# When the 64-column products with V are issued: two attention stages of a diffusion trunk on one core

## The chip, the cores and the metric

The kernel runs on one core of one Trainium2 chip. Its time is the time of the whole program on the device in microseconds (us). The kernel before took 2924.12 us, the median of 3 runs (2918.45 to 2926.39).

## The reference, cut to what matters

Two transformer layers work on 1024 latent tokens and 256 context tokens of width 1024, all in float32. Each layer has an attention mixer and a gated feed-forward part. Layer 0 has windowed attention with 16 query heads that share 4 key heads, layer 1 has neighbourhood attention with 16 heads and a bias. In both, the head width is 64, and the part that the change touches is the last line, p times V:

```
# layer 0: a block of 128 queries sees 3 blocks of latent keys and the 256 context keys
s = einsum('bqhgd,bkhd->bhgqk', q_b, k_b) * scale
p = softmax_f32(where(valid, s, NEG_INF), sink_g)
o = einsum('bhgqk,bkhd->bqhgd', p, v_b)
# layer 1: the same with a window in two dimensions and a bias on the scores
s_lat = einsum('bjqhd,bjkhd->bhjqk', q_b, k_s) * scale + bias
s_ctx = einsum('bjqhd,bkhd->bhjqk', q_b, k_c) * scale
p = softmax_f32(where(valid, concatenate([s_lat, s_ctx], -1), NEG_INF))
o = einsum('bhjqk,bjkhd->bjqhd', p[..., :nkey], v_s) + einsum('bhjqk,bkhd->bjqhd', p[..., nkey:], v_c)
```

## The kernel before, in words

The program has five stages, one after the other: projections of layer 0 (`front0`), its attention (`attn0`), output projection and feed-forward part (`back`), the projections of layer 1 (`front1`), its attention (`attn1`), and `back` again. The change touches the two attentions. Everything outside them is products of 128 by 128 weights.

Both attentions work through units. A unit of the first one is a key head g and a block b of 128 queries, with the four query heads that share that key head: 4 times 10 units. A unit of the second one is a pair of heads and a block m of 128 queries: 8 times 8 units. A unit goes through four steps:

- `begin` loads the queries of the unit into a buffer (`qst`). The first attention has 2 such buffers and uses one a unit, with four DMAs (L543, L544). The second one loads two query blocks at a time, for the two heads apart, into 3 buffers (L679 to L682); a load waits until the scores have read what the buffer held. All these DMAs go out in order on SyncE's queue, among the loads of keys, V, bias and weights.
- `scores` multiplies queries and keys into two banks of PSUM (L555 and L557; L697 and L700), of which there are two pairs. VectorE adds mask or bias and takes the minimum (L564; L705), which frees the banks, and ScalarE takes the exponential (L569; L707).
- `turn` transposes the exponentials on TensorE, 128 keys at a time (L588; L725), and copies the result from PSUM to SBUF on VectorE or ScalarE in turn (L509 or L511) into a tile `pt` or `ptt`.
- `finish` multiplies those tiles by V (L598; L740). V has 64 columns a head, so such a product fills half the columns of TensorE; a product for the upper 64 rows of the output and one for the lower 64 stand beside each other in the code. The trace has two MATMUL records for each of these products. After them the reciprocals of the sums are turned to the same layout (L601; L746), the result is scaled and split into two parts for the output projection.

The units overlap: in one turn of the loop the code writes the scores of unit u, the transposes of the unit before it (`prev`), and then `finish`, in the first attention of `prev`, in the second of the unit before `prev` (`old`).

The order on each engine is not the order of the code. A scheduler builds it when the program is built: among the instructions whose inputs are ready by its own reckoning it takes the one written first. `tc.high_priority(offset=n)` lets what stands in it count as if it were written n instructions earlier; the scores have 10 and 20 (HP0, HP1). So the products of `finish` are dealt out one by one where the scheduler finds room between transposes and scores. On the chip each engine follows its list in order and waits where an input is late.

Of the kernel before, what the change touches and what calls it, by code (L numbers as in the profile page):

```python
# [11 lines left out]
F32 = mybir.dt.float32  # L12
# [7 lines left out]
P = 128  # L20
# [9 lines left out]
EPS = 1e-6  # L30
HP0 = 10
HP1 = 20
MB1 = 1
ST, SB = "sq", 1
SP = ((1, 0), (0, 1))
# [13 lines left out]
def f32(ap):  # L49
    return ap.bitcast(F32)  # L50


class Trunk:
# [459 lines left out]
    def attn0(self):  # L513
        nc, tc, a = self.nc, self.tc, self.a
        with ExitStack() as cx:
# [2 lines left out]
            cx.enter_context(self.early)  # L518
            pool = self.early_pool
            late = self.pool(cx, "at0l", 1)  # L520
            prt = lambda: late.tile([P, 640], F32, name="pr0", tag="pr0", bufs=9)
            ptile = lambda: late.tile([P, 512], F32, name="pt", tag="pt", bufs=8)
            o = [self.pair_tiles(c) for c in range(3)]
            mask, mask7 = (self.slot(F32).rearrange("p a n -> p (a n)")[:, :n] for n in (640, 512))
            sink = pool.tile([P, HEADS], F32, name="sink", bufs=1)
# [5 lines left out]
            def load_g(g):  # L531
                kst = pool.tile([P, T], F32R, name="kst")
                for i in range(2):
                    nc.sync.dma_start(out=f32(kst[64 * i:64 * i + 64]), in_=f32(self.ks[0][g * 64:(g + 1) * 64, i, :]))
                v = pool.tile([P, 10, DH], F32, name="vg")
                nc.sync.dma_start(out=v, in_=self.vs[0][0, :, g * 64:(g + 1) * 64].rearrange("(t p) d -> p t d", p=P))
                return kst, v

            def begin(g, b, kst, v):
                q = pool.tile([P, 2, 4, P], F32R, name="qst", tag="qst", bufs=2)  # L540
                for i in range(2):
                    s = f32(self.qs[0][g * 256:(g + 1) * 256, i, b * P:(b + 1) * P]).rearrange("(h d) t -> d h t", d=DH)
                    nc.sync.dma_start(out=f32(q[0:64, i]), in_=s)  # L543
                    nc.sync.dma_start(out=f32(q[64:128, i]), in_=s)  # L544
                lat = list(range(max(b - 1, 0), min(b + 2, 8))) if b < 8 else []
                return dict(g=g, b=b, kst=kst, v=v, q=q, kts=lat + [8, 9], nl=len(lat) * P, p=[], pt=[],
                            sm=self.small.tile([P, 4], F32, name="sm"), mn=self.small.tile([P, 4], F32, name="mn4"))
# [37 lines left out]
            def turn(u, i):  # L585
                tp = self.bank()
                for h in range(4):
                    nc.tensor.transpose(tp[:, h * P:(h + 1) * P], u["p"][h][:, i * P:(i + 1) * P], self.ident)  # L588
                pt = ptile()
                self.evac(pt, tp)  # L590
                u["pt"].append(pt)

            def finish(u):
                g, b, kts = u["g"], u["b"], u["kts"]
                op = self.bank()
                for i, kt in enumerate(kts):
                    for r in range(2):
                        nc.tensor.matmul(op[64 * r:64 * r + 64, :256], u["v"][:, kt, :], u["pt"][i][:, 256 * r:256 * r + 256],  # L598
                                         start=(i == 0), stop=(i == len(kts) - 1))
                for x in range(2):  # L600
                    nc.tensor.transpose(op[:, 256 + x * P:256 + (x + 1) * P], u["rx"][:, x * P:(x + 1) * P], self.ident)  # L601
                ot = late.tile([P, 256], F32, name="ot0", tag="ot0")
                nc.scalar.copy(out=ot, in_=op[:, 256:512])
                nc.vector.tensor_tensor(out=ot, in0=op[:, :256], in1=ot, op=ALU.mult)  # L604
                if b < 8:
                    ov = ot.rearrange("p (x m j) -> p x m j", x=2, m=8)
                    for c in range(2):
                        oh, ol = (o[c][i][g].rearrange("p x (m t) -> p x m t", t=P)[:, :, :, b * 16:b * 16 + 16]
                                  for i in range(2))
                        sv = ov[:, :, 4 * c:4 * c + 4]  # L610
                        nc.gpsimd.tensor_copy(out=oh, in_=sv)
                        nc.gpsimd.tensor_tensor(out=ol, in0=sv, in1=f32(oh), op=ALU.subtract)
                else:
                    oh, ol = (o[2][i][g][:, :, (b - 8) * P:(b - 7) * P] for i in range(2))
                    sv = ot.rearrange("p (x j) -> p x j", x=2)
                    nc.gpsimd.tensor_copy(out=oh, in_=sv)
                    nc.gpsimd.tensor_tensor(out=ol, in0=sv, in1=f32(oh), op=ALU.subtract)

            prev = None
            for g in range(4):  # L620
                kst, v = load_g(g)
                for b in ORD:
                    if WB(g, b):
                        self.wo_ahead.append(self.unit(a["w_o0"][len(self.wo_ahead)], LO, after=prev["rx"] if len(self.wo_ahead) < 2 else None))
                    u = begin(g, b, kst, v)
                    n = len(prev["kts"]) if prev else 0
                    for j in range(max(4, n)):
                        if j < 4:
                            with tc.high_priority(offset=HP0):
                                scores(u, j)  # L630
                        if j < n:
                            turn(prev, j)
                    if g == 0 and b == RB:
                        self.rest(ptile)
                    if prev:
                        finish(prev)
                    prev = u
            for j in range(len(prev["kts"])):
                turn(prev, j)
            finish(prev)  # L640
        return o

    def attn1(self):
        nc, tc, a = self.nc, self.tc, self.a
        with ExitStack() as cx:
# [3 lines left out]
            late = self.pool(cx, "at1l", 1)  # L649
            prt = lambda: late.tile([P, 640], F32, name="pr1", tag="pr1", bufs=4)  # L650
# [39 lines left out]
            def scores(u, x):  # L690
# [19 lines left out]
                if m % 2 == 1 and x == 1:  # L710
# [5 lines left out]
                    u["rx"] = rx  # L716
                    if m == MB1:
                        cur["rx"] = rx
# [12 lines left out]
            def finish(u):  # L731
                pr, m, kts = u["pr"], u["m"], u["kts"]
                if m % 2 == 0:
                    u["two"]["op"] = self.bank()
                op = u["two"]["op"]
                ov = op[:, (m % 2) * P:(m % 2) * P + P]
                n = len(kts)
                for i in range(n):
                    for x in range(2):
                        nc.tensor.matmul(ov[64 * x:64 * x + 64, :], u["v"][:, kts[i], 64 * x:64 * x + 64],  # L740
                                         u["pt"][i // 2][:, (2 * (i % 2) + x) * P:(2 * (i % 2) + x + 1) * P],
                                         start=(i == 0), stop=(i == n - 1))
                if m % 2 == 0:
                    return
                for y in range(2):
                    nc.tensor.transpose(op[:, 256 + y * P:256 + (y + 1) * P], u["rx"][:, y * P:(y + 1) * P], self.ident)  # L746
                ot = late.tile([P, 256], F32, name="ot1", tag="ot1")
                nc.scalar.copy(out=ot, in_=op[:, 256:512])
                nc.vector.tensor_tensor(out=ot, in0=op[:, :256], in1=ot, op=ALU.mult)
                c0 = (m % 4 - 1) * P  # L750
                oh, ol = (o[m // 4][i][pr // 2][:, pr % 2, c0:c0 + 256] for i in range(2))
                nc.scalar.copy(out=oh, in_=ot)
                nc.gpsimd.tensor_tensor(out=ol, in0=ot, in1=f32(oh), op=ALU.subtract)

            old = prev = None
            for pr in range(8):
                load_pair(pr)
                for m in range(8):
                    if m % 2 == 1 and pr == 7:
                        self.wo_ahead.append(self.unit(a["w_o1"][len(self.wo_ahead)]))  # L760
                    u = begin(pr, m)
                    steps = list(range(0, len(prev["kts"]), 2)) if prev else []
                    for j in range(max(2, len(steps))):
                        if j < 2:
                            with tc.high_priority(offset=HP1):
                                scores(u, j)
                        if j < len(steps):
                            turn(prev, steps[j])
                    if old:
                        finish(old)  # L770
                    old, prev = prev, u
            for i in range(0, len(prev["kts"]), 2):
                turn(prev, i)
            finish(old)
            finish(prev)
        return o

# [498 lines left out]
```

## Time and profile before

| | |
|---|---|
| time of the profiled execution | 2916.41 us |
| its span, from the first to the last instruction | 2914.6 us |
| TensorE (PE) busy | 2840.7 us, 97% of the span, 15586 MATMUL records |
| VectorE (DVE) busy | 1642.0 us, 56% |
| ScalarE (ACT) busy | 1123.9 us, 39% |
| GpSimd (POOL) busy | 790.9 us, 27% |
| granted TensorE clock, mean | 0.994 |
| first attention | about 278 to 548 us of the span |
| second attention | about 1883 to 2149 us |

A MATMUL record reaches from its start to the modelled end of its result; neighbours overlap, so a busy share of 97% says that TensorE is nearly always at something, not that it is at its peak. What a stream of products costs is read from the distance between starts.

### The profile page before, as it was taken

The page shows a single profiled execution, that of the slowest core. Times are in us where ns is not written, and L with a number is a line of the kernel's source. Part 1 is how long each engine was busy: PE and PEld are TensorE (multiplying, and loading weights), DVE is VectorE, ACT ScalarE, POOL GpSimd, SP SyncE. Part 2 cuts the span into 40 slices and gives each one's busy share as a digit, 9 for nine tenths or more (in the row PEclk, how much of TensorE's full clock was granted, in tenths as well). Part 3 has the DMA queues.
Part 4 walks back from the last instruction along what each step waited for, and adds up shares of the span by engine and source line. Part 5 has one row for each costly group of instructions (what it writes and reads, how often), then busy time and mean ns, then how long its engine had stood idle before and what let it go on. Part 6 is the DMA issues. An engine that isn't in the chain of part 4 may idle for free.

```text
span 2914.6 us, 42716 instructions
## 1 busy us (share of the span) xinstructions
PE 2840.7 (97%) x15586; PEld 2303.1 (79%) x15586; DVE 1642.0 (56%) x2965; ACT 1123.9 (39%) x2263; POOL 790.9 (27%) x802
## 2 busy tenths in 40 slices
PE   6999999999999999999999999999999999999999
PEld 3667777787888887778998888777788788887887
DVE  5667777558665644446543444266656965566442
ACT  4323666435232322224543223266644522233120
POOL 3443242110122122233872345011101021223220
PEclk8999999999999999999999999999999999999999
DMA  7573342433322258544552554356654422226221
GB/s 267 191 233 95 98 130 73 164 110 131 127 85 86 76 176 287 179 160 140 186 185 89 148 160 127 110 158 158 180 171 136 145 91 82 85 85 204 87 91 62
DMA packets 306178, 404.18 MB, mean 139 GB/s; under 512 B 30128, under 2 KB 165808, under 8 KB 305968
## 3 DMA queue, kind: packets, MB, share of 16 engines
q1 hardware_dynamic: 237072, 362.91, 39.3%
q10 hardware_dynamic: 68896, 38.55, 4.6%
q8 instruction: 123, 2.02, 0.3%
q14 instruction: 87, 0.71, 0.1%
HBM read 317.73 MB, written 83.62 MB: 138 GB/s over the span
## 4 chain that ended last, share of the span: by engine, by line
PE 86%; DVE 3%; DMA 2%; issue 1%; POOL 1%; ACT 1%; SPq 0%; DVEq 0%; ACTq 0%; POOLq 0%
PE b L802 16%; PE bm L1062 16%; PE bm L802 11%; PE bm L352 11%; PE bm L860 7%; PE bm L1123 4%; PE b L598 3%; PE b L588 3%; PE b L740 2%; PE b L1062 2%; PE b L725 2%; PE b L352 2%; DMA qst<-q_s 1%; PE b L555 1%; PE b L697 1%; PE b L700 1%
## 5 line engine op out<-in xcount | busy, mean ns | idle before, releaser
L1062 PE MATMUL bm<-pr,wsp 128*128 128x512 f32 x1920 | 440.3, 390 | 0.0
L1062 PEld LDWEIGHTS bm<-pr,wsp 128*128 128x128 f32 x1920 | 359.3, 188 | 82.0 <-issue 5.9
L802 PE MATMUL b<-wsp,px 128*128 128x512 f32 x1584 | 377.2, 391 | 0.0
L802 PEld LDWEIGHTS b<-wsp,px 128*128 128x128 f32 x1584 | 297.5, 188 | 65.1
L802 PE MATMUL bm<-pr,px 128*128 128x512 f32 x1296 | 316.6, 392 | 5.4 <-ACT kp L964 5.2
L842 DVE SCALAR_TENSOR_TENSOR px<-bm,mod,px 128x512 f32<-128x512 f32 (+1 forms) x232 | 170.3, 739 | 268.4 <-PE bm L1062 219.7
L141 ACT CAST wsp<-raw 128x512 fp32r<-128x512 f32 x306 | 188.0, 620 | 341.1 <-PE bm L1062 122.2
L802 PEld LDWEIGHTS bm<-pr,px 128*128 128x128 f32 x1296 | 243.3, 188 | 59.7 <-ACT kp L964 6.1
L352 PE MATMUL bm<-wsp,pr 128*128 128x512 f32 x1152 | 272.4, 393 | 0.0
L142 POOL TENSOR_TENSOR px<-wt,px 128x512 fp32r<-128x512 f32 x64 | 91.3, 1427 | 626.6 <-ACT px L141 383.4
L352 PEld LDWEIGHTS bm<-wsp,pr 128*128 128x128 f32 x1152 | 213.4, 188 | 43.4
L142 POOL TENSOR_TENSOR wsp<-raw,wsp 128x512 fp32r<-128x512 f32 x132 | 174.9, 1333 | 249.0 <-ACT wsp L141 224.5
L141 ACT CAST px<-wt 128x512 fp32r<-128x512 f32 x176 | 107.9, 621 | 334.5 <-PE b L802 301.8
L142 DVE TENSOR_TENSOR wsp<-raw,wsp 128x512 fp32r<-128x512 f32 x174 | 140.4, 812 | 145.7 <-ACT wsp L141 145.5
L860 PE MATMUL bm<-pr,wsp 128*128 128x512 f32 x768 | 176.8, 390 | 1.0 <-DVE ot L604 1.0
L860 PEld LDWEIGHTS bm<-pr,wsp 128*128 128x128 f32 x768 | 143.3, 188 | 30.5 <-DVE ot L604 1.2
L352 PE MATMUL b<-wsp,pr 128*128 128x512 f32 x576 | 149.3, 414 | 18.3 <-ACT pr L261 6.6
L705 DVE CUSTOM_DVE_ANT_0 pr<-b,wsp,big 128x640 f32<-128x640 f32 (+1 forms) x128 | 107.4, 846 | 87.1 <-PE b L700 86.0
L352 PEld LDWEIGHTS b<-wsp,pr 128*128 128x128 f32 x576 | 110.9, 198 | 55.6 <-issue 9.9
L292 POOL TENSOR_TENSOR hrs<-hss,mhalf 128x8 f32<-128x8 f32 (+1 forms) x66 | 104.7, 1586 | 167.7 <-DVE hss L290 162.8
L1160 DVE TENSOR_TENSOR t<-b,kp 128x512 f32<-128x512 f32 x88 | 60.7, 690 | 135.3 <-PE b L802 133.9
L1123 PE MATMUL bm<-prc,wsp 128*128 128x256 f32 x1056 | 134.2, 285 | 0.0
(205 smaller groups left out, 4834.7 us busy)
## 6 DMA issues: line engine op xcount, KB each, us to landing
raw<-w_gu SPq DMA_DIRECT2D x156, 256.0 KB, 2.8
qst<-q_s SPq DMA_DIRECT2D x288, 128.0 KB, 3.1
rawf<-w_gu SPq DMA_DIRECT2D x132, 256.0 KB, 3.0
raw<-w_down SPq DMA_DIRECT2D x110, 256.0 KB, 3.3
wsp<-w_ada SPq DMA_DIRECT2D x48, 512.0 KB, 7.0
pr<-w_ada SPq DMA_DIRECT2D x48, 512.0 KB, 6.4
s_s<-t SPq DMA_DIRECT2D x88, 256.0 KB, 2.0
rawf<-s_s SPq DMA_DIRECT2D x88, 256.0 KB, 3.1
```

What stands on the lines that cost most here:

```text
L141: self.nc.scalar.copy(out=w[:, 0, :n], in_=x)
L142: getattr(self.nc, lo).tensor_tensor(out=w[:, 1, :n], in0=x, in1=f32(w[:, 0, :n]), op=ALU.subtract)
L292: nc.gpsimd.tensor_tensor(out=rs[:, :nh], in0=ss[:, :nh], in1=self.mhalf[:, :nh], op=ALU.pow)
L352: self.nc.tensor.matmul(ps, x, y, start=(k == 0 and i == 0), stop=(k == KT - 1 and i == 2))
L588: nc.tensor.transpose(tp[:, h * P:(h + 1) * P], u["p"][h][:, i * P:(i + 1) * P], self.ident)
L598: nc.tensor.matmul(op[64 * r:64 * r + 64, :256], u["v"][:, kt, :], u["pt"][i][:, 256 * r:256 * r + 256], start=(i == 0), stop=(i == len(kt ...
L705: nc.vector.tensor_tensor_reduce(out=pt[:, :nl + 256], in0=V, in1=u["bias"][x][m // 7][:, b0:b0 + nl + 256], scale=-1.0, scalar=self.big, ...
L802: self.nc.tensor.matmul(ps, x, y, start=first and k == 0 and i == 0, stop=last and k == 3 and i == 2, skip_group_check=True)
L842: nc.vector.scalar_tensor_tensor(out=h[c, k], in0=ps, scalar=mod[:, ty, k, z:z + 1], in1=h[c, k], op0=ALU.mult, op1=ALU.add)
L860: nc.tensor.matmul(ps[:, :n], x, y, start=(k == 0 and i == 0), stop=(k == KT - 1 and i == 2))
L1062: nc.tensor.matmul(ps, x, y, start=(z == 0 and i == 0), stop=(z == len(parts) - 1 and i == 2))
L1123: nc.tensor.matmul(ps[:, q * CTX:(q + 1) * CTX], x, y, start=(k == 0 and i == 0), stop=(k == KT - 1 and i == 2))
```

## The change

There are four parts.

- In the first attention the products with V of a unit stand in `high_priority(offset=HV0)` with HV0 = 0.
- `finish` of the first attention comes one unit later, as in the second one (`done`), and at the end two of them follow each other. As the tiles `pt` live one unit longer, there are 10 of them and not 8; of the tiles with exponentials (`pr0`) there are 8 and not 9.
- In the second attention the products stand in `high_priority(offset=HV1)` with HV1 = 100.
- There the blocks of keys are taken in reverse, the last one first.

Number and shapes of all instructions stay as they were.

```
-            prt = lambda: late.tile([P, 640], F32, name="pr0", tag="pr0", bufs=9)
-            ptile = lambda: late.tile([P, 512], F32, name="pt", tag="pt", bufs=8)
+            prt = lambda: late.tile([P, 640], F32, name="pr0", tag="pr0", bufs=8)
+            ptile = lambda: late.tile([P, 512], F32, name="pt", tag="pt", bufs=10)
...
-                for i, kt in enumerate(kts):
-                    for r in range(2):
-                        nc.tensor.matmul(op[64 * r:64 * r + 64, :256], u["v"][:, kt, :], u["pt"][i][:, 256 * r:256 * r + 256],
-                                         start=(i == 0), stop=(i == len(kts) - 1))
+                n = len(kts)
+                with tc.high_priority(offset=HV0):
+                    for i in range(n):
+                        for r in range(2):
+                            nc.tensor.matmul(op[64 * r:64 * r + 64, :256], u["v"][:, kts[i], :], u["pt"][i][:, 256 * r:256 * r + 256],
+                                             start=(i == 0), stop=(i == n - 1))
...
-                    if prev:
-                        finish(prev)
-                    prev = u
+                    if done:
+                        finish(done)
+                    done, prev = prev, u
             for j in range(len(prev["kts"])):
                 turn(prev, j)
+            finish(done)
             finish(prev)
...
-                for i in range(n):
-                    for x in range(2):
-                        nc.tensor.matmul(ov[64 * x:64 * x + 64, :], u["v"][:, kts[i], 64 * x:64 * x + 64],
-                                         u["pt"][i // 2][:, (2 * (i % 2) + x) * P:(2 * (i % 2) + x + 1) * P],
-                                         start=(i == 0), stop=(i == n - 1))
+                with tc.high_priority(offset=HV1):
+                    for i in reversed(range(n)):
+                        for x in range(2):
+                            nc.tensor.matmul(ov[64 * x:64 * x + 64, :], u["v"][:, kts[i], 64 * x:64 * x + 64],
+                                             u["pt"][i // 2][:, (2 * (i % 2) + x) * P:(2 * (i % 2) + x + 1) * P],
+                                             start=(i == n - 1), stop=(i == 0))
```

What the scheduler makes of it is seen on TensorE. In the rows of an order, b is a bank of PSUM, pt and ptt are transposed exponentials, pr holds exponentials, vg and v hold V, ident is the identity of a transpose, and rx the reciprocals; x8 says that eight such instructions follow each other. The first place is on TensorE in the first attention, the last query block of the first key head, whose eight products go into one bank (b_3360 before). Before:

```order
L598 MATMUL b_3360<-pt,vg 64x256 x4
L588 MATMUL b_3393<-ident,pr_3297 128x128
L588 MATMUL b_3393<-ident,pr_3312 128x128
L598 MATMUL b_3360<-pt,vg 64x256 x2
L588 MATMUL b_3408<-ident,pr_3297 128x128
L588 MATMUL b_3408<-ident,pr_3312 128x128
L555 MATMUL b_3385<-kst,qst 128x384 x2
...
L588 MATMUL b_3408<-ident,pr_3327 128x128
L598 MATMUL b_3360<-pt,vg 64x256 x2
L601 MATMUL b_3360<-ident,rx_3244 128x128 x2
```

And now the same unit (its bank is b_3435, and line 598 is line 602 of the changed kernel):

```order
L590 MATMUL b_3428<-ident,pr_3322 128x128
L557 MATMUL b_3397<-kst,qst 128x384 x2
L559 MATMUL b_3397<-kst,qst 128x256 x2
L557 MATMUL b_3412<-kst,qst 128x384 x2
L559 MATMUL b_3412<-kst,qst 128x256 x2
L602 MATMUL b_3435<-pt,vg 64x256 x8
L605 MATMUL b_3435<-ident,rx_3232 128x128 x2
```

The three groups of four, two and two products have become one of eight, and the reciprocals follow at once.

The second place is on TensorE in the second attention, between two score products: L700 into b_19629 is the last to read a query buffer, and L697 into b_19710 is the first that needs what is loaded into that buffer. Before:

```order
L700 MATMUL b_19629<-kst_19457,qst_19576 128x384 x2
L740 MATMUL b_19620<-ptt,v_19455 64x128 x8
L697 MATMUL b_19645<-kst_19466,qst_19579 128x256 x2
L700 MATMUL b_19645<-kst_19466,qst_19579 128x384 x2
L725 MATMUL b_19638<-ident,pr_19589 128x128
L740 MATMUL b_19620<-ptt,v_19455 64x128 x4
L725 MATMUL b_19658<-ident,pr_19589 128x128
L740 MATMUL b_19620<-ptt,v_19455 64x128 x3
L725 MATMUL b_19665<-ident,pr_19589 128x128
L740 MATMUL b_19620<-ptt,v_19455 64x128 x2
...
L740 MATMUL b_19620<-ptt,v_19455 64x128
...
L697 MATMUL b_19710<-kst_19466,qst_19690 128x256 x2
```

And now:

```order
L705 MATMUL b_19629<-kst_19457,qst_19576 128x384 x2
L746 MATMUL b_19620<-ptt,v_19455 64x128 x8
L702 MATMUL b_19645<-kst_19466,qst_19579 128x256 x2
L705 MATMUL b_19645<-kst_19466,qst_19579 128x384 x2
L730 MATMUL b_19638<-ident,pr_19589 128x128
L730 MATMUL b_19658<-ident,pr_19589 128x128
L746 MATMUL b_19620<-ptt,v_19455 64x128 x10
...
L752 MATMUL b_19620<-ident,rx_19552 128x128 x2
L702 MATMUL b_19710<-kst_19466,qst_19690 128x256 x2
```

The same eighteen products stand between the two score products in two groups and not in five, and no group has an odd number.

In the whole program the 336 products of the first attention stand in 105 groups before and in 48 now, the 608 of the second in 130 before and 67 now. Groups with an odd number of products: none before and 16 now in the first, 54 before and none now in the second. Outside the attentions some sixty instructions of each `back` change places with neighbours of the same kind.

## Rows read from the trace of the kernel before

**Rows 1.** The page: busy time of each engine, share of the span, instructions

```profile
PE 2840.7 (97%) x15586; PEld 2303.1 (79%) x15586; DVE 1642.0 (56%) x2965; ACT 1123.9 (39%) x2263; POOL 790.9 (27%) x802
```

**Rows 2.** By stretch: us; busy PE, PEld, DVE, ACT, POOL (records); clock; DMA share, GB/s

```profile
278.00:548.00 270.00, 264.91 (x1950) 194.38 (x1950) 195.91 (x548) 184.98 (x483) 82.74 (x195) 1.00 0.34 96
1883.00:2149.00 266.00, 257.79 (x2362) 207.33 (x2360) 171.20 (x407) 169.84 (x408) 38.14 (x86) 0.99 0.59 155
2112.80:2117.00 4.20, 4.19 (x36) 3.85 (x36) 2.14 (x4) 1.78 (x6) 0.73 (x1) 0.59 0.51 176
```

**Rows 3.** Timeline of TensorE, first attention: start, duration, records, waits in brackets

```profile
339.71 1.08 PE L598 MATMUL b<-pt,vg 128*64 128x256 f32 x8
340.73 0.44 PE L588 MATMUL b<-ident,pr 128*128 128x128 f32 x2
341.10 0.65 PE L598 MATMUL b<-pt,vg 128*64 128x256 f32 x4
341.68 0.44 PE L588 MATMUL b<-ident,pr 128*128 128x128 f32 x2
```

**Rows 4.** Timeline of TensorE and one query load, second attention

```profile
2018.53 1.09 PE L740 MATMUL b<-ptt,v 128*64 128x128 f32 x16
2018.63 0.52 SPq L681 DMA_DIRECT2D qst<-q_s  x1
...
2019.55 0.51 PE L697 MATMUL b<-kst,qst 128*128 128x256 f32 x2
...
2020.25 0.27 PE L725 MATMUL b<-ident,pr 128*128 128x128 f32 x1
2020.45 0.66 PE L740 MATMUL b<-ptt,v 128*64 128x128 f32 x8
...
2021.04 0.33 PE L725 MATMUL b<-ident,pr 128*128 128x128 f32 x1
2021.30 0.65 PE L740 MATMUL b<-ptt,v 128*64 128x128 f32 x6
...
2021.88 0.33 PE L725 MATMUL b<-ident,pr 128*128 128x128 f32 x1
2022.14 0.44 PE L740 MATMUL b<-ptt,v 128*64 128x128 f32 x4
2022.51 0.39 PE L697 MATMUL b<-kst,qst 128*128 128x256 f32 x1
2022.73 0.93 PE L725 MATMUL b<-ident,pr 128*128 128x128 f32 x7
2023.41 0.36 PE L697 MATMUL b<-kst,qst 128*128 128x256 f32 x1
...
2024.06 0.43 PE L740 MATMUL b<-ptt,v 128*64 128x128 f32 x2
2024.43 0.44 PE L746 MATMUL b<-ident,rx 128*128 128x128 f32 x2
2026.25 0.47 PE L697 MATMUL b<-kst,qst 128*128 128x256 f32 x2 [1.39 <-DMA qst<-q_s]
```

**Rows 5.** Who TensorE waited for, whole run: us, times, longest

```profile
PE b L697 <- DMA qst<-q_s: 8.1, 9, 1.9
...
PE b L555 <- DVE mn L564: 1.5, 7, 0.4
```

**Rows 6.** Timeline, one query load of the second attention that was quick

```profile
1878.16 0.52 SPq L681 DMA_DIRECT2D qst<-q_s  x1
...
1881.74 0.47 PE L697 MATMUL b<-kst,qst 128*128 128x256 f32 x2 [0.93 <-DMA qst<-q_s]
```

**Rows 7.** Timeline, one query load of the first attention

```profile
369.26 0.57 SPq L543 DMA_DIRECT2D qst<-q_s  x1
...
376.39 0.71 PE L555 MATMUL b<-kst,qst 128*128 128x384 f32 x2
```

**Rows 8.** Timeline of TensorE, the longest wait for queries

```profile
2112.81 0.58 PE L697 MATMUL b<-kst,qst 128*128 128x256 f32 x2 [1.94 <-DMA qst<-q_s]
```

More of the change, by code (lines that the diff above doesn't have):

```diff
@@ L32 @@
 HP1 = 20
+HV0 = 0
+HV1 = 100
 MB1 = 1
@@ L617, in finish @@
                     nc.gpsimd.tensor_tensor(out=ol, in0=sv, in1=f32(oh), op=ALU.subtract)
-            prev = None
+            done = prev = None
             for g in range(4):
```

## The prediction

> **What bounds the kernel now.** The page comes first: TensorE is busy 97% of the span, VectorE 56% [rows 1]. That is a mean over stages, so the second view is the busy time by stretch [rows 2]: TensorE works 264.9 of the 270 us of the first attention and 257.8 of the 266 us of the second, at a granted clock of 1.00 and 0.99. VectorE is at 196 of 270 and 171 of 266 there, ScalarE close behind. So TensorE sets the pace in both, and whatever shortens its list shortens the kernel, less what it then has to wait for. The third view is the timeline of TensorE, read by the distances between starts [rows 3, 4], because the durations of records overlap. The reader is to see there that the same work costs more in small groups. The fourth is who TensorE waits for [rows 5]: in the second attention the loads of queries (9 waits, 8.1 us), in the first the minimum on VectorE that frees the score banks (7 waits, 1.5 us).
>
> **What one break in the products costs.** In the second attention [rows 4] a group of 16 records takes 2019.55 - 2018.53 = 1.02 us up to the next instruction, a group of 8 takes 0.59. Eight records more are 0.43 us, so 0.054 each, and the group of 8 carries 0.59 - 0.43 = 0.16 us that do not depend on its length. The instructions at its ends pay too. Seven transposes in a row take 0.68 us with a last step of 0.03 (the score product slips in early), so one is 0.11. A lone transpose ahead of products takes 0.20 (2020.25 to 2020.45), 0.09 more; one that also follows products takes 0.26 (2021.04 to 2021.30), another 0.06 more. A break thus costs 0.16 + 0.09 + 0.06 = 0.31 us. In the first attention [rows 3] 8 records take 1.02 and 4 take 0.58: 0.44 for four, 0.14 fixed. The two transposes between take 0.37 and not 0.22, which is 0.15 more; 0.29 in all. I take 0.30 us for each group.
>
> An odd group pays once more: 6 records take 0.58 us where 8 take 0.59, and 2 take 0.37 where 4 take 0.37 [rows 4]. The product without a partner costs as much as a pair, and the waste is half a pair, 0.11 us. The first attention has no odd group before; a pair there is 0.44 us [rows 3], so its waste lies between 0 and 0.22 us, and I take 0.22, since the second attention shows the full half.
>
> Here a rule of the Trainium skill can be set against the rows. "TensorEngine Tiling (Array Packing)", section "Key Properties", says that a change of tiling mode drains TensorE, and "TensorE: Matmul & The Clock Gate", "Step-by-step: what each phase is for", puts a drain at about 128 cycles. An estimate from these pages: 53 ns at 2.4 GHz, two changes a group, 0.11 us a group, a third of what the rows show. By it the gain of the next part would be 12.6 us from the groups in place of 36, and the waits below would eat it all. The trace agrees with the rule that a change costs, not with its size, and the measurement decides.
>
> **The change part by part.** Counted in the order: the groups go from 105 to 48 in the first attention and from 130 to 67 in the second.
> - First attention: 57 groups fewer by 0.30 us, 17.1 us less; 16 new odd groups by 0.22, 3.5 us more. Net 13.6 us less.
> - Second: 63 fewer by 0.30, 18.9 us less; 54 odd groups gone by 0.11, 5.9 us less. Net 24.8 us less.
>
> That is 38 us less work in TensorE's list. Nothing else in it changes but the order. What is late next:
>
> *Query loads, second attention.* A load starts when the scores have read the buffer, and the score that needs it follows some microseconds of TensorE work later. Nine times TensorE stands waiting already [rows 5], and what is saved in front of such a wait is no gain. In the place of [rows 4] the load is issued at 2018.63 and the score starts at 2026.25, after 1.39 us of waiting. In the new order three groups and two odd ones are gone between the two score products, 1.1 to 1.3 us, and the wait grows by that. I went through the 31 loads of this kind in the order with the prices above. The two like this one lose 1.3 and 1.45 us, seven at or near a change of head pair 0.1 to 0.6 and 2.3 together, one that had its data just in time begins to wait 1.3, and two near the end lose 1.4 us of the waits they have. Together the waits grow by 5 us, and each holds all that stands behind it in TensorE's list. Bounds: nothing if loads start that much earlier, 15 us if every load took half a microsecond longer with loads closer together (the quickest took 3.6 us from issue to use [rows 6], that of [rows 4] 7.6).
>
> *Query loads, first attention.* There the products move a unit back, so the first units have less work between. The load of [rows 7] was issued at 369.26 and its score ran at 376.39, without a wait but with none to spare. By the order and the prices the work between is 3.2 us shorter, so that the score waits 3.2 us; the first load of the stage that has to wait for a buffer loses 1.6 and one more 0.5; four others come within 0.25 us of being late. I take 5 us, bounds 0 and 9.
>
> *Score banks, first attention.* With the products in one piece the scores stand closer together. If I give the minimum on VectorE 1.1 us from the scores to the free bank, the order has 17 places before, and 38 now, where the scores after next come sooner. The 7 waits named take 0.2 us each, the longest 0.4 [rows 5]. 21 more by 0.2 are 4 us; bounds 0 and 8.
>
> *No cost, and why.* The copies that fill the tiles for the products: between the last transpose of a block and the products the new order has at least 1.2 us of TensorE work in the second attention and over 3 us in the first, and a unit at the end cannot wait for long. The 8 tiles of exponentials: only the first two scores of the stage need a tile less than 2.5 us after its last reader, at most 0.6 us. The DMAs on SyncE's queue keep their number; four bias loads move together behind a query load. Two results in a row at the end of the first attention: GpSimd has 82.7 us of work in 270 [rows 2]. The swapped products in `back` are of one kind: nothing.
>
> **Sum.** 38 less 5, 5 and 4 leaves 24 us. The profiled execution took 2916.41 us (its span is 2914.6), so 2892. It lies 7.7 us below the median of the runs before, 2924.12, and the changed kernel will be timed as those were; I forecast 2924 - 24 = 2900 us.
>
> **The rivals.**
> 1. *All of it arrives.* If loads and minima shift along with TensorE, only a few microseconds are lost: 2924 - 35 = 2889 us, at best 2885. For it: VectorE has a quarter of each stage free [rows 2]. Against it: a load that starts when TensorE frees a buffer takes its own time.
> 2. *No gain in the end.* VectorE and ScalarE, at 73% and 69% in the first attention, and the loads take over the pace, so that the waits swallow some 30 of the 38 us: 2916 to 2924. For it: the 21 closer score places. Against it: 5 and 8 us of idle TensorE in the two stages [rows 2], not a sign of another engine near its end.
> 3. *Slower: the query loads of the second attention become the pace.* There are 31 whose score comes soon after the buffer is free; now 5.4 us of TensorE work lie between on average and in the new order 4.8. If each took 7.0 us, close to the slow one of [rows 4], the waits would be 31 x (7.0 - 4.8), some 67 us against 9 now: 58 more against 38 saved, 2944 us. The point from which it decides is a mean load of 6.4 us, where 38 us are lost. For it: the DMA share is 0.59 in this stage [rows 2]. Against it: the present mean, by landings, is 4.9. It would also cost clock: after the wait of 1.94 us at 2112.81 [rows 8] the granted clock was 0.59 over 4.2 us [rows 2], four fifths of it at the lower level of 1.2 GHz, about 1.7 us lost.
>
> **How the numbers follow.** A difference of less than 0.3% (8.8 us) cannot be told from no change by a measurement of this kernel. Forecast, 14 to 34 us gained: 0.62. Rival 1: 0.20. Rival 2: 0.13. Rival 3: 0.05. Faster takes the first two and a little of the second rival's edge, 0.84; same 0.11; slower 0.05. The likeliest one's own range is 2890 to 2910. The range reaches to the full gain with a run some microseconds lower than the median (2882) and into the second rival (2916).
>
> **What would show it.** In the profile after: some 48 and 67 groups, 0.30 us fixed for each; the first attention 5 to 12 us shorter, the second 17 to 22; waits of L697's successor for queries of about 13 us; no change in the other stages. I am wrong if the groups are fewer and the stages as long as before, or if the waits for queries or for the minimum exceed 25 us.

## The result, and the profile after

The changed kernel takes 2892.44 us, the median of 4 runs (2890.35 to 2896.47), against 2921.65 for the kernel before in 4 runs beside it: a ratio of 0.990 with a 95% interval of 0.988 to 0.992, about 29 us less (25 to 35 by the interval). The profiled execution took 2896.47 us, its span is 2894.7. It is the slowest of its four, and that of before was the fastest of its own, so the two traces lie only 20 us apart.

The prediction was 2900 us with a range of 2882 to 2916. Stage by stage, from the first score product of an attention to the first product of the output projection behind it:

| us | until the first score | first attention | between | second attention | rest |
|---|---|---|---|---|---|
| before | 267.3 | 282.7 | 1324.5 | 274.6 | 765.5 |
| after | 269.8 | 279.0 | 1325.3 | 254.3 | 766.2 |

The stages that the change leaves alone agree within a microsecond or so, the first one apart: it took 267 to 274 us in the executions profiled for this study, though its code is the same in all. A single profile cannot weigh five microseconds, so the medians stand beside it below.

The page of the changed kernel, busy time as in [rows 1]. TensorE's is 29 us less for the same number of records:

```profile
PE 2812.0 (97%) x15586; PEld 2310.6 (80%) x15586; DVE 1645.7 (57%) x2965; ACT 1119.7 (39%) x2263; POOL 791.0 (27%) x802
```

By stretch, columns as in [rows 2]. The first two rows are the attentions; the other two are pieces of the first one, and the only ones of 10 us between 278 and 548 with a clock below 1.00 (before there was none):

```profile
278.00:548.00 270.00, 262.21 (x1965) 206.91 (x1965) 199.91 (x554) 185.40 (x489) 81.80 (x193) 0.99 0.36 98
1874.00:2128.00 254.00, 238.01 (x2398) 207.04 (x2398) 176.13 (x419) 172.17 (x419) 40.22 (x91) 1.00 0.62 166
...
368.00:378.00 10.00, 7.96 (x47) 7.11 (x47) 6.80 (x17) 9.00 (x21) 5.17 (x8) 0.83 0.45 137
388.00:398.00 10.00, 7.48 (x46) 4.47 (x47) 5.00 (x14) 5.09 (x15) 5.61 (x10) 0.83 0.59 178
```

The place of [rows 4] in the second attention (L681 is now L686, L697 L702, L700 L705, L725 L730, L740 L746, L746 L752):

```profile
2007.36 0.52 PE L705 MATMUL b<-kst,qst 128*128 128x384 f32 x2
2007.80 1.09 PE L746 MATMUL b<-ptt,v 128*64 128x128 f32 x16
2007.90 0.52 SPq L686 DMA_DIRECT2D qst<-q_s  x1
...
2008.83 0.51 PE L702 MATMUL b<-kst,qst 128*128 128x256 f32 x2
...
2009.52 0.38 PE L730 MATMUL b<-ident,pr 128*128 128x128 f32 x2
2009.83 1.31 PE L746 MATMUL b<-ptt,v 128*64 128x128 f32 x20
...
2012.64 0.38 PE L752 MATMUL b<-ident,rx 128*128 128x128 f32 x2
2014.58 0.47 PE L702 MATMUL b<-kst,qst 128*128 128x256 f32 x2 [1.56 <-DMA qst<-q_s]
```

There are two groups between the score products and no single one at the end. From the first group to the score's start it is 6.78 us, and 7.72 before: 0.94 us gained, although the wait for queries, 1.56 us, stands in the same place. The load was issued at 2007.90 and used 6.7 us later; before it was 7.6.

Who TensorE waited for, whole run, as in [rows 5]:

```profile
PE b L702 <- DMA qst<-q_s: 11.7, 12, 2.1
...
PE b L559 <- ACT pr L571: 2.2, 1, 2.2
...
PE b L590 <- ACT pt L513: 1.8, 5, 1.2
...
PE b L702 <- DVE ot L755: 1.2, 1, 1.2
...
PE b L590 <- ACT pr L571: 0.9, 1, 0.9
...
PE b L590 <- DVE pt L511: 0.6, 1, 0.6
PE b L557 <- DMA qst<-q_s: 0.6, 1, 0.6
...
PE b L557 <- DVE mn L566: 0.5, 3, 0.2
```

In the first attention TensorE waits for queries once, 0.6 us, and for the minimum 0.5 us where it was 1.5. What is new there are the waits for exponentials (`pr`), which ScalarE writes: 2.2 and 0.9 us, and none in the kernel before. The timeline of the longest such wait (L143 prepares a weight of the output projection, L571 is the exponential, L559 the score product that needs its bank):

```profile
390.30 1.30 ACT L143 CAST wsp<-raw 128x512 fp32r<-128x512 f32 x2 [2.26 <-DMA raw<-w_o]
...
391.50 0.47 ACT L571 ACTIVATE pr<-b,mn 128x256 f32<-128x256 f32 x1
...
392.11 0.56 PE L559 MATMUL b<-kst,qst 128*128 128x256 f32 x2 [2.16 <-ACT pr L571]
```

ScalarE stood 2.26 us for a weight that had not landed, the exponential stood behind it, and TensorE behind that. Other waits are too short for the table. A transpose needs its exponentials and a new bank of PSUM, and a bank is free once its copy is done. TensorE's weight loads (PEld) where a bank is late:

```profile
317.08 0.90 PEld L590 LDWEIGHTS b<-ident,pr 128*128 128x128 f32 x8
...
317.60 0.58 ACT L513 COPY pt<-b 128x512 f32<-128x512 f32 x1 [1.14 <-PE b L590]
...
318.24 0.42 PEld L590 LDWEIGHTS b<-ident,pr 128*128 128x128 f32 x4 [0.26 <-ACT pt L513]
```

I counted the steps from one transpose to the next where a third stands ahead of them. Before, 6 of 393 took over 0.13 us and held 0.6 us beyond the usual 0.11. After, it is 40 of 479, with 5.1 us (one long wait in each trace left out). By the releasers of the trace 2.8 of the 5.1 us are waits for copies, 1.6 for exponentials, 0.4 are four steps at half clock and 0.4 the rest.

The copies did not become dearer, though. Before the change TensorE waited for them elsewhere, at transposes that follow score products, which this count leaves out. The kernel before in the first attention, TensorE and its weight loads:

```profile
PE b L588 <- ACT pt L511: 2.0, 4, 1.6
PE b L588 <- DVE pt L509: 0.6, 3, 0.2
...
PEld b L588 <- ACT pr L569: 0.4, 1, 0.4
```

Named waits for copies are 2.6 us there and 2.4 in the changed kernel. What grew is the waits for exponentials. In the changed kernel the weight loads wait for them:

```profile
PEld b L590 <- ACT pr L571: 3.4, 9, 1.1
PEld b L559 <- ACT pr L571: 2.4, 1, 2.4
```

To weigh the short waits too, every step of TensorE in the stage, from one start to the next, is set against the usual step between the same kinds of instructions, and what is over it is put down to its releaser. The usual steps added up, with what odd groups waste, are the list. Copies then cost 5.1 us before and 5.4 after, exponentials 0.4 and 6.0. It is the same in the four other traces with the new order in this stage (copies 4.8 to 5.4, exponentials 4.6 to 5.4) and in the three others with the old one (copies 4.3 to 5.4, exponentials 0.1).

### The profile page after: what moved, and what is told of

Same layout as the page of the kernel before. It is cut to its first block, busy times and chain, and to the rows that moved or that the text cites. A ratio compares the mean times of both kernels' runs of the same rounds, so it can differ in the third digit from the quotient of the medians.

```text
span 2894.7 us, 42717 instructions
## 1 busy us (share of the span) xinstructions
PE 2812.0 (97%) x15586; PEld 2310.6 (80%) x15586; DVE 1645.7 (57%) x2965; ACT 1119.7 (39%) x2263; POOL 791.0 (27%) x802
## 4 chain that ended last, share of the span: by engine, by line
PE 87%; DMA 4%; DVE 4%; ACT 1%; issue 1%; POOL 1%; SPq 1%; DVEq 0%; ACTq 0%; POOLq 0%
PE b L808 17%; PE bm L1068 16%; PE bm L808 12%; PE bm L354 11%; PE bm L866 7%; PE bm L1129 4%; PE b L602 3%; PE b L354 3%; PE b L590 2%; PE b L1068 2%; DMA qst<-q_s 2%; PE b L730 2%; PE b L746 2%; PE b L557 1%; PE b L161 1%
## 5 line engine op out<-in xcount | busy, mean ns | idle before, releaser
L143 ACT CAST wsp<-raw 128x512 fp32r<-128x512 f32 x306 | 188.3, 620 | 342.5 <-PE bm L1068 116.3
L143 ACT CAST px<-wt 128x512 fp32r<-128x512 f32 x176 | 108.3, 621 | 330.5 <-PE b L808 302.4
```

The source lines that it names most:

```text
L143: self.nc.scalar.copy(out=w[:, 0, :n], in_=x)
```

## The experiments

Each median stands against runs of the kernel before that were timed beside it, 2922.5 to 2924.4 us; "groups" are counted in the order, odd ones in brackets. The stage times are those of one profiled execution.

| | groups first | groups second | median us | ratio (95%) | first attention us | second us |
|---|---|---|---|---|---|---|
| second_only | 105 (0) | 66 (0) | 2906.9 | 0.995 (0.993-0.996) | 283.5 | 258.2 |
| first_only | 48 (16) | 132 (50) | 2915.5 | 0.997 (0.996-0.998) | 278.1 | 273.7 |
| wide | 105 (0) | 95 (48) | 2907.8 | 0.995 (0.993-0.996) | 284.0 | 261.0 |
| worse_order | 48 (16) | 135 (78) | 2910.3 | 0.996 (0.995-0.998) | 276.6 | 272.7 |
| forward | 48 (16) | 87 (0) | 2909.4 | 0.995 (0.994-0.997) | 277.8 | 272.3 |
| four_buffers | 48 (16) | 64 (0) | 2880.7 | 0.986 (0.984-0.987) | 274.5 | 241.5 |
| buffer_alone | 105 (0) | 146 (72) | 2919.9 | 0.999 (0.998-1.000) | 282.9 | 273.5 |
| whole_runs | 40 (0) | 67 (0) | 2898.0 | 0.991 (0.990-0.993) | 279.6 | 253.5 |
| no_weights_ahead | 47 (14) | 67 (0) | 2897.6 | 0.991 (0.990-0.992) | 275.0 | 256.5 |
| both_better | 40 (0) | 64 (0) | 2889.8 | 0.988 (0.987-0.989) | 281.4 | 242.8 |
| split_copies | 44 (8) | 66 (0) | 2920.5 | 0.999 (0.998-1.000) | 302.1 | 261.6 |

**Each half alone.** `second_only` is the changed kernel with the first attention as before, `first_only` the other way round.

> The change in the second attention alone; the first as before. Theory (a break in the 64-column products costs TensorE 0.30 us, a lone product half a pair): 66 groups and none odd as in the changed kernel, so the second attention takes 254 us as there (274.6 before), and the whole is 20 us faster than before. Rival (the two parts need each other, or the gain of the medians, 29 us, sits mostly in the first): 10 us or less.

> The change in the first attention alone; the second as before (132 groups, 50 odd). Theory: 12 to 14 us less in TensorE's list of the first attention and 8 to 10 us more waiting there, so the stage is 3 to 5 us shorter (282.7 before) and the whole 4 us faster, which is within what can't be told from no change. Rival (the medians are right and the two profiles understate it): 9 us faster.

The halves gained 17.5 and 8.9 us by their medians, 26 together against 29 for both. The second attention came to 258.2 us, 4 more than the expected 254; its waits for queries were 13.0 us in 15, close to the 13 predicted. The first attention gained 4.6 us in its trace and about 9 in the median, so the rival's 9 cannot be turned down on that side. The traces that bear on it are compared below.

**Is it the break, or the 64 columns?** `wide` is the kernel before with one product of 128 columns for the two of 64:

```
-                    for x in range(2):
-                        nc.tensor.matmul(ov[64 * x:64 * x + 64, :], u["v"][:, kts[i], 64 * x:64 * x + 64], ...
+                    nc.tensor.matmul(ov, u["v"][:, kts[i], :], u["pt"][i // 2][:, 2 * (i % 2) * P:(2 * (i % 2) + 1) * P], ...
```

> The kernel before, with the products of the second attention made 128 columns wide: one product with both heads of V in place of the two of 64 columns, so that the array is never divided there. It leaves out the second head's weights (both halves use the first head's). 304 products of 0.218 us take the place of 304 pairs of 0.218 us, in 95 groups, 48 of them odd. Theory (the price of a break is that of changing between 64 and 128 columns): the distances between starts at the ends of a group are the plain ones, 130 x 0.30 + 54 x 0.11 = 45 us leave the list, and with 10 to 15 us more waiting for queries the stage takes 240 to 248 us. Rival (any other kind of instruction in between costs as much, another bank or another operand): 95 groups still cost 0.30 us each, only 16 us leave the list, and the stage takes 258 to 262 us.

Two groups in its timeline, each with the instruction that follows:

```profile
2012.27 0.61 PE L739 MATMUL b<-ptt,v 128*128 128x128 f32 x4
2012.72 0.38 PE L744 MATMUL b<-ident,rx 128*128 128x128 f32 x2
...
2016.87 1.05 PE L739 MATMUL b<-ptt,v 128*128 128x128 f32 x8
2017.76 0.93 PE L725 MATMUL b<-ident,pr 128*128 128x128 f32 x7
```

Four records take 0.45 us up to the next instruction and eight take 0.89: 0.11 each, and nothing is left over for the ends. A transpose ahead of a group or behind one takes 0.11 too, and a group with an odd number of products loses nothing. So a break as such costs nothing; the 0.30 us are the price of going from 128 columns to 64 and back. The Trainium skill has the direction: in "TensorEngine Tiling (Array Packing)", section "Key Properties", a change of tiling mode drains TensorE. The trace agrees with that, and its size stays the 0.30 us of the rows.

The stage time alone would have misled: 261.0 us lies in the rival's range. By the usual steps the list of the stage is 212 us and was 256, so 44 us left it, where the theory has 45 and the rival 16. TensorE's busy time fell from 263.5 us (of 1875 to 2149) to 237.4. More than half of the gain went back into waits for queries (27.3 us, 8.1 before), a lower clock (0.97 on average) and other waits:

```profile
1875.00:2145.00 270.00, 237.41 (x1833) 225.33 (x1832) 176.56 (x420) 176.46 (x423) 40.08 (x92) 0.97 0.59 158
```

```profile
PE b L697 <- DMA qst<-q_s: 27.3, 21, 3.7
```

**Offset and direction in the second attention.** In `worse_order` HV1 is 0; `forward` takes `range(n)` in place of `reversed(range(n))`.

> The changed kernel with an offset of 0 in place of 100 in the second attention: the scheduler then deals the products out in 135 groups, 78 of them odd, with the same instructions. Theory: 68 groups by 0.30 and 78 odd ones by 0.11 are 29 us more in the list than in the changed kernel, less some 5 us of waits for queries that they hide; the stage takes 276 to 284 us (254 in the changed kernel, 274.6 before), the whole is at 2914 to 2920. Rival (what helps is the reversed order of the blocks, or that the products wait for nothing): the stage stays below 262 us, as the blocks are reversed here too.

> The changed kernel with the key blocks of the second attention taken in order, the first one first, instead of reversed. Its products stand in 87 groups and not 67, none odd. Theory: 20 groups by 0.30 us are 6 us more in the list, of which some waits for queries hide up to 3: the stage 257 to 260 us, the kernel 2895 to 2899. Rival: the reversal matters for more than the count, since in the forward order the first products of a unit could start on tiles filled long ago and the last of them waits for the copy that is written last; then waits for copies of ptt show in the second attention and the stage is over 262 us.

`worse_order` gave back 18.4 us of the stage for 68 groups and 78 odd ones more, 29 us by the prices; its waits for queries fell to 2.1 us from 11.7, so these had hidden a third of the list. The gain comes from the order, as the theory has it, though 272.7 us is 3 us below its range: the waits that hide a longer list were 9.6 us, not 5.

`forward` missed both expectations. It lost 18.0 us with 20 groups more, and of the waits for copies that the rival names one came, 1.1 us at a score product. The windows and waits of its second attention:

```profile
1871.00:2143.50 272.50, 248.63 (x2393) 210.50 (x2393) 177.44 (x419) 175.76 (x419) 39.39 (x91) 0.98 0.59 155
```

```profile
PE b L702 <- DMA qst<-q_s: 16.2, 10, 2.8
PE b L702 <- DVE ot L755: 3.7, 3, 1.4
```

Named waits grew by 8.0 us (23.8 against 15.8), three pieces of 10 us had a clock of 0.83 where after has none, about 1.7 us each, and the groups are 6.0: 19 of the 18. One of the three, the clock in its fourth column from the end:

```profile
1922.00:1924.00 2.00, 2.00 (x15) 1.97 (x15) 1.15 (x3) 0.89 (x3) 0.00 (x0) 0.80 0.08 29
1924.00:1925.00 1.00, 1.00 (x5) 0.69 (x4) 0.43 (x1) 0.82 (x2) 0.74 (x1) 0.50 0.00 0
```

It lies behind a wait of 2.27 us for queries that ended at 1921.81. So the reversal is worth more than its 20 groups; why TensorE waits longer for loads in forward order is open.

**The buffers for queries.** `four_buffers` is the changed kernel with `bufs=4` and not 3 for `qst1`, `buffer_alone` the kernel before with the same.

> The changed kernel with 4 query buffers in the second attention in place of 3; 64 groups, none odd. Theory (what the second attention still loses is the wait for query loads that begin only when a buffer is read out, 11.7 us in 12 waits): with a buffer more, the load for the second head begins a unit earlier and the waits fall below 3 us, so the stage takes 243 to 247 us (254.3 in the changed kernel) and the whole is 9 us faster than the changed kernel, at 2883. Rival (the DMA queue or SyncE's order makes the queries late, not the buffer): waits and time as in the changed kernel.

> The kernel before with four buffers for the queries of the second attention in place of three, and nothing else; the products with V stand in 146 groups there (130 before), 72 of them odd (54 before). Theory: what the buffer takes away are the waits for queries, some 9 us in this stage, and the 16 groups more at 0.30 us and 18 odd ones more at 0.11 us cost 6.8, so the second attention comes from 274.6 to about 272 us and the kernel gains 2 to 3 us: within 0.3% of before. In the changed kernel the same buffer took 12 us, because its list was already short and loads were what was late. Rival: the buffer is worth as much here as it was there, 12 us, the stage about 262 us, and the gain of the two is simply a sum.

`four_buffers` has no wait for queries left; the second attention takes 241.5 us, 1.5 less than expected, and the kernel 2880.7 us, the fastest of all. What TensorE still waits for in that stage:

```profile
PE b L746 <- ACT ptt L513: 2.3, 1, 2.3
PE b L702 <- DMA kst<-k_s: 1.6, 4, 1.0
PE b L702 <- DVE mn L710: 1.1, 2, 0.9
```

The same buffer alone gains 2.6 us (0.1%), since the scheduler spreads the products over 146 groups when queries come early. The gain of the two is not a sum: the buffer pays only with the new order.

**The first attention.** `whole_runs` has HV0 = 100, `both_better` adds the fourth buffer of the second attention, and `no_weights_ahead` prepares no weights of the output projection during the stage (`WB = lambda g, b: False`).

> The changed kernel with the products of the first attention at an offset of 100 in place of 0: 40 groups and none odd there, 48 and 16 odd in the changed kernel. Theory: 8 x 0.30 + 16 x 0.22 = 5.9 us less in the list of the first attention, of which a part is lost to waits: the stage takes 272 to 276 us (276.6 to 279.0 with the order of the changed kernel), the whole is 2 to 5 us faster than the changed kernel. Rival (the first attention is now held by ScalarE and VectorE): no shorter.

> The changed kernel with 4 query buffers in the second attention and the offset of 100 in the first: 40 and 64 groups, none odd. Theory: the two gains add, 11 to 14 us faster than the changed kernel, 2878 to 2882. Rival: as the changed kernel, 2892.

> The changed kernel without the six units of output weights that the first attention loads and splits ahead of time; they are loaded when the output projection needs them. 47 groups, 14 odd. Theory (the gain that the first attention lost went to casts of these weights, which stand in ScalarE's list ahead of exponentials and copies and wait for their DMA, 5.9 us in 3 waits): the waits of TensorE for exponentials and copies in that stage (4.9 us in 7 waits) shrink to 2 us and the stage takes 271 to 274 us; the projection after it gets longer by 0 to 6 us. Rival (the waits come from the order of scores and products itself): the stage stays at 276 to 279 us.

Eight groups and 16 odd ones fewer are 5.9 us off the list, and the first attention of `whole_runs` is no shorter, 279.6 us. Its waits there:

```profile
PE b L557 <- DMA qst<-q_s: 5.3, 5, 2.0
PE b L590 <- ACT pr L571: 3.7, 7, 2.7
```

The rival's time holds, its cause only in small part: what leaves TensorE's list turns into waits for queries, 5.3 us against 0.6 in the changed kernel. Waits for exponentials are much as they were there (2.2 and 0.9 us). This stage has two buffers for queries; a third was not tried. `both_better` repeats it: 281.4 us, and 9 us slower than `four_buffers`, so the two gains do not add. Without the weights ahead the waits for ScalarE fell to 1.1 us from 4.9, and the stage took 275.0. In it TensorE stood 4.4 us behind the first score product for an operand (`hx`) that VectorE still had to write, and 2.0 us in after:

```profile
PE b L557 <- DVE hx L298: 4.4, 1, 4.4
```

Without these 2.4 us the stage would be at 272.6, in the range of the theory. But orders equal to that of after took 274.5 to 279.0, and the whole gained nothing. So the weights explain single long waits; what they cost the stage stays open.

**Copies out of PSUM.** `split_copies` makes each copy of the first attention in two halves at once:

```
-                self.evac(pt, tp)
+                nc.vector.tensor_copy(out=pt[:, :256], in_=tp[:, :256])
+                nc.scalar.copy(out=pt[:, 256:], in_=tp[:, 256:])
```

> The changed kernel, in whose first attention each copy of four transposes from PSUM is made in two halves at once, 256 columns on VectorE and 256 on ScalarE, in place of 512 columns on the one or the other in turn. What is to be tested: in the trace of the changed kernel 40 steps between transposes that follow transposes are over 0.13 us, 5.1 us together beyond the usual 0.11 (before the change 6 such steps, 0.6 us), each of them where a bank still waits for its copy (0.58 us on ScalarE, 0.68 on VectorE). Theory: transposes that are no longer parted by products outrun the copies, so half copies (0.37 us by a copy of 128x256 on ScalarE in this stage) free the banks sooner and the steps over 0.13 us hold less than 2 us; the new order has 44 groups and not 48, 8 odd and not 16, which is 2.9 us less by itself; the stage comes to 269 to 272 us (274.5 to 279.0 in the executions so far). Rival: ScalarE, which gets 84 more copies and 13 us more work here, delays exponentials and copies alike, the steps over 0.13 us stay at 4 us or more, and waits for ScalarE grow: the stage 275 us or more.

The expectation put all of the 40 steps down to copies; by the releasers 2.8 of their 5.1 us are, and the waits for copies were hardly longer than before the change. The rival holds, and by more than it said: the stage takes 302.1 us and the gain of the whole change is gone. The short steps stayed, 50 with 4.3 us, and long waits for ScalarE's copies came on top, with a clock of 0.87 behind them:

```profile
PE b L590 <- ACT pt L593: 10.3, 17, 2.2
...
PE b L557 <- DVE mn L566: 2.9, 7, 1.9
```

```profile
400.00:440.00 40.00, 37.26 (x253) 29.12 (x252) 25.30 (x78) 22.89 (x67) 10.66 (x28) 0.87 0.37 99
```

The waits show that the stage cannot take more copies on ScalarE, which is 69% busy in after. How much of the 23 us comes from its 13 us more of work, and how much from tiles that now wait for both engines, this run does not part. The second attention, whose code is untouched, took 261.6 us here, 7 more than in after, with 14.6 us of waits for queries; this I cannot explain.

## Why the prediction was right, point by point

*The price of a break* held. The groups in the trace of after cost what those of before did: 16 records take 1.03 us up to the next instruction (2007.80 to 2008.83; 1.02 before), and 20 take 1.24 or 1.25, which is the fixed 0.16 and 20 by 0.054. `wide` shows that the price belongs to the change of columns. *The odd group* in the first attention was bounded by 0 and 0.22 us. Ten records:

```profile
361.70 1.51 PE L602 MATMUL b<-pt,vg 128*64 128x256 f32 x10
363.14 0.62 PE L557 MATMUL b<-kst,qst 128*128 128x384 f32 x2
```

take 1.44 us. By the steps of [rows 3] eight take 1.02 and twelve 1.46: the lone product costs a whole pair, and 0.22 was right.

*The second attention* held in size and cause: predicted 24.8 us off the list less 5 of waits, measured 20.3. The waits for queries grew from 8.1 to 11.7 us, all named waits of the stage from 10.6 to 15.8. At [rows 4] I expected the wait to grow by 1.3 us; it grew by 0.17, as the load took 0.9 us less, and other places made up for part of it: 3.6 us in all where 5 were forecast.

*The first attention* came out near the forecast by errors that cancel. Predicted: 13.6 off the list, 5 back for queries, 4 back for score banks, 4.6 net. By the steps of the two traces some 13.8 left the list and 10.1 came back, 3.7 net:

| us beyond the usual steps | before | after | predicted change |
|---|---|---|---|
| exponentials (ScalarE) | 0.4 | 6.0 | none named |
| lower clock | 1.0 | 4.1 | none named |
| queries | 0.0 | 1.2 | 5 |
| minimum (score banks) | 4.8 | 5.4 | 4 |
| copies out of PSUM | 5.1 | 5.4 | 0 |
| results | 1.6 | 0.8 | 0 |

These rows add up to 9.8 of the 10.1 us. The prediction had looked at the copies and not at the exponentials, the other thing that a transpose waits for, and it had no clock term in this stage. It had also named the minimum (1.5 us) as what TensorE waits for there, though the copies of ScalarE, 2.0 us in 4 waits, stood above it. The added low clock is the two pieces of 10 us at 0.83, each 3.4 us at half speed, so 1.7 lost; one stands behind the wait of 2.16 us shown above, the other behind one of 1.18 us for a copy and one of 0.86 us for an exponential, both on ScalarE. Why queries took so much less than 5 is not shown; loads that shift along with TensorE, as in rival 1, would fit. The sign of "5 to 12 us shorter" did not come in this trace. In the five traces with the new order the stage takes 274.5 to 279.0 us, 277.2 on average, in the four with the old one 282.7 to 284.0, 283.3 on average: 6.1 us gained, and the fastest, `four_buffers`, has neither of the two low pieces. So the pair of profiles understates this stage, though the 6.1 us rest on nine single executions.

*The sum.* 24 us were forecast; the profiled executions give 20, the medians 29, with an interval of 25 to 35. The difference lies within what the first stage (267 to 274 us) and the first attention (274.5 to 279.0) vary between executions. So the forecast was a little low.

*The rivals.* All of it arriving (35 us) is not out by the time, since 2892 lies between its 2889 and the forecast. It is out by the traces: the named waits of the second attention grew by 5.2 us, and in the first 10 of 13.8 us came back. `four_buffers` gained 12 us more, with the waits for queries gone. No gain in the end is out for the change, but it is what `whole_runs` met one step further. The slower one, queries as the pace, is out with 67 groups; `wide`, with a still shorter list, is where it begins: 21 waits, 27.3 us, a clock of 0.97.

## What to carry to other kernels

Read the price of a group from the distances between starts: products of half the columns cost 0.30 us for each time they are taken up, and half a pair if their number is odd, so keep them in few and even runs. When the list of the bounding engine gets shorter, ask what each piece that moves had been covering: here loads of queries, and in the first attention the time that ScalarE needs for exponentials. And when a count of waits looks at one kind of place, look at the places that it leaves out before calling a wait new: the copies out of PSUM had only moved. Then give what is late next another buffer in the same step: order alone gained 29 us, the buffer alone 3, both 42 (medians).

## What the runs showed that was not expected

- Products of 128 columns can be broken up at no cost (0.11 us a step throughout, in groups of 4 and 8 records); with 64 columns a break costs 0.30 us.
- A wait of TensorE of about 2 us is often followed by some 3.4 us at the lower clock level of 1.2 GHz (0.50 in 1924 to 1925 of `forward`), so that it costs nearly twice its length: so after the waits of 2.27, 1.84 and 2.78 us in `forward` and of 2.16 us at 392.11 in after. Not always: the wait of 2.05 us at 2078.84 in after left the clock at 1.00.
- Halving the copies, with 13 us more of work on a ScalarE that is busy 69%, made the stage 23 us longer (`split_copies`).
